# Hybrid diffusion step on one core: the low parts and sums of the feed-forward stages, sums of squares and rope product move from GpSimd to VectorE

## The chip, the cores and the metric

The kernel runs on one core of a Trainium2 chip. The metric is the device time of one execution in microseconds (us). A core has TensorE (PE, matrix products), VectorE (DVE), ScalarE (ACT), GpSimd (POOL) and SyncE (SP), which here only issues transfers. Each engine takes its instructions in a fixed order and waits at the head of its own queue.

## The reference

Two layers (DEPTH 2, width 1024) run over 256 context tokens and 1024 latent tokens. Each layer mixes attention, a recurrent unit and a long convolution, then a SwiGLU feed-forward of width 2816. Cut to what the change touches:

```python
def trunk_layer(x, mod, lp, ctx):
    sh1, sc1, g1, sh2, sc2, g2 = mod
    h = rmsnorm(x, lp['norm1_w']) * (1 + sc1) + sh1
    p = h @ lp['w_in']
    q = rmsnorm(p[..., :OFF_K].reshape(B, L, N_HEADS, HEAD_DIM), lp['q_norm_w'])
    k = rmsnorm(p[..., OFF_K:OFF_V].reshape(B, L, N_KV, HEAD_DIM), lp['k_norm_w'])
    ...
    q, k = axial_rope(q), axial_rope(k)      # latent tokens only
    ...
    x = x + g1 * (mix @ lp['w_out'])
    h2 = rmsnorm(x, lp['norm2_w']) * (1 + sc2) + sh2
    x = x + g2 * ((jax.nn.silu(h2 @ lp['ffn_w1']) * (h2 @ lp['ffn_w3'])) @ lp['ffn_w2'])
```

All data is float32.

## The kernel before

A float32 product is made of three products of reduced-precision parts (`mm3`, L154 to L156): high by high, high by low, low by high. Each operand is therefore cut in two: ScalarE copies the high part (`split`, L160, or L527), and a subtraction gives the low part (L161, or L528). Which engine subtracts is an argument. "Cut" below means such a pair, and in counts its subtraction.

The latent tokens are two blocks of 512. The feed-forward uses a fast 2x2 block scheme with seven products in place of eight. It has three pieces in each layer.

- `quarters` makes the seven operands: the normalised blocks (scaled at L507), their sums and differences (L538, L539, L546, L547), and a cut of each (`hq` holds both parts or the high ones, `hl` the low parts of three of them).
- `ffn_up` loops over 11 pairs p of weight tiles, with two parts each (w1 and w3). A part loads two `wst` tiles, cuts them and their differences into four `whl` tiles of 128x1024, makes seven products `pu` for the latent tokens and two `puv` for the context, evacuates them on VectorE (L622, L637 to L648) and applies the gate. At the end of a pair five block sums (L656) go to memory (L657); those that are named `gs` share one buffer.
- `ffn_down` runs seven stages over 11 steps each. A step loads one or two quarters of w2 into `wst` (L694), adds two at L706 where there are two, cuts the result into `whl`, loads and cuts the stored sum `gr`, and multiplies. Stages 1 and 3 (from 0) also serve the context: two more weight cuts (`C`) and one of the context's `gr` half, `gk`. Stages end with the update of `x_l` (L733).

`ss_add` (L353) adds squares for the norms, the sums with index h = 1 on GpSimd. `head_norm` (L776) normalises q and k and applies the rope: shuffle (L804), product (L805), two more steps.

Weight tiles share pools: four `whl` buffers and three `wst` buffers. The order of every engine's instructions is set by a scheduler from the order of the code and its own costs, so the change of an engine can also move other instructions.

Of the kernel before, what the change touches and what calls it, by code (L numbers as in the profile page):

```python
# [11 lines left out]
F32 = mybir.dt.float32  # L12
# [3 lines left out]
ALU = mybir.AluOpType  # L16
# [72 lines left out]
class Net:  # L89
# [261 lines left out]
    def ss_add(self, s, pool, ss, xs, d, three=3):  # L351
        nc = self.nc
        if d < 2:  # L353
            nc.scalar.activation(ss[:, d], xs, AF.Square)
        else:
            if s.lat:
                sq = pool.tile(list(xs.shape), F32, tag=self.sq[0], name="sq", bufs=self.sq[1])
            else:
                sq = self.rows(list(xs.shape))
            nc.scalar.activation(sq, xs, AF.Square)  # L360
            h = 0 if d % three == 0 else 1
            (nc.gpsimd if h else nc.vector).tensor_tensor(ss[:, h], ss[:, h], sq, ALU.add)

    def h_new(self, s, bi, hp):
        s.h[bi] = []
# [144 lines left out]
    def quarters(self, cp, cq, hp):  # L510


        nc = self.nc
        ha, hb, _ = hp
        b11, b21 = self.lat.x[0]
        b12, b22 = self.lat.x[1]
        V, G = nc.vector, nc.gpsimd

        def pair(p, tag):
            t = p.tile([128, 2, 4, 512], F32R, tag=tag, name="hq")  # L520
            return t[:, 0], t[:, 1]

        def low(tag):
            return cp.tile([128, 4, 512], F32R, tag=tag, name="hl")

        def cut(x, hl, k, eng):
            nc.scalar.activation(hl[0][:, k], x[:, k], AF.Copy)  # L527
            eng.tensor_tensor(hl[1][:, k], x[:, k], hl[0][:, k].bitcast(F32), ALU.subtract)  # L528

        h11, h21 = pair(hb, "hl00"), pair(ha, "hl01")  # L530
        for k in range(4):
            cut(b11, h11, k, G)
            cut(b21, h21, k, V)
        t1, h22 = pair(hb, "hl10"), pair(hb, "hl11")
        a, b = pair(cq, "hq1")
        c = cq.tile([128, 4, 512], F32R, tag="hq4", name="hq4")
        for k in range(4):
            V.tensor_tensor(b11[:, k], b12[:, k], b11[:, k], ALU.subtract)  # L538
            V.tensor_tensor(b12[:, k], b22[:, k], b12[:, k], ALU.subtract)  # L539
            cut(b11, t1, k, G)  # L540
        t3 = (a, low("xq00"))
        for k in range(4):
            cut(b12, t3, k, V if k % 2 else G)
        for k in range(4):
            cut(b22, h22, k, G)
            V.tensor_tensor(b22[:, k], b22[:, k], b11[:, k], ALU.subtract)  # L546
            V.tensor_tensor(b21[:, k], b22[:, k], b21[:, k], ALU.subtract)  # L547
        t2 = (b, low("xq10"))
        for k in range(4):
            cut(b22, t2, k, V)  # L550
        t4 = (c, low("xq11"))
        for k in range(4):
            cut(b21, t4, k, V if k % 2 else G)
        return h11, h21, h22, t4, t1, t2, t3

    def ffn_up(self, l, pool, cp, hq, mods):


        nc, a = self.nc, self.a
        H = NFF // 2  # L560
        lat, cs = self.lat, self.ctxs
        V, G = nc.vector, nc.gpsimd
        h11, h21, h22, t4, t1, t2, t3 = hq
        e = cp.tile([128, 4, 512], F32, tag="xq01", name="e")

        def cut(st):
            w = self.wp.tile([128, 2, 8, 128], F32R, tag="whl", name="whl", bufs=WBUFS)
            self.split(st, w[:, 0], w[:, 1], G)
            return w

        def prod(w, x, b):
# [5 lines left out]
        for p in range(H):  # L577
            ts = {}
            cps = [None, None]
            for part, src in enumerate((a["ffn_w1"][l], a["ffn_w3"][l])):  # L580
                raw = []
                for i in range(2):
                    f = p + i * H
                    st = self.wp.tile([128, 8, 128], F32, tag="wst", name="wst", bufs=SBUFS)
# [65 lines left out]
            for q, (b, op) in enumerate(BSUM):  # L650
                if len(b) == 1:
                    t = ts[b[0]]
                else:
                    n = q % 3
                    t = e[:, n + 1] if n else pool.tile([128, 512], F32, tag="gs", name="gs", bufs=1)
                    G.tensor_tensor(t, ts[b[0]], ts[b[1]], op)  # L656
                nc.sync.dma_start(lat.gd[q, p], t)  # L657
            for m in mods[2 * p:2 * p + 2]:
                self.mods(*m, self.rows, lambda nm, shp=(128, 512): self.ps_l(nm, shp, "n"))
# [1 line left out]
    def ffn_down(self, l, hp, pool, xp, last):  # L661

        nc, a = self.nc, self.a
# [20 lines left out]
        for n, (quads, op, q, outs, ctx, nxt) in enumerate(DOWN):  # L684
# [3 lines left out]
            for p in range(H):  # L688
# [12 lines left out]
                if ctx:  # L701
                    C = self.wp.tile([128, 2, 2, 512], F32R, tag="whl", name="whl", bufs=WBUFS)
                    for j in range(2):
                        self.split(st[:, j], C[:, j, 0], C[:, j, 1], nc.gpsimd)
                if len(src) == 2:
                    nc.vector.tensor_tensor(st[:, 0], st[:, 0], st[:, 1], op)  # L706
                self.split(st[:, 0], A[:, 0], A[:, 1], nc.gpsimd)
                self.split(br, B[:, 0], B[:, 1], nc.vector)
                if n < 2 and 0 < p < 9:
                    if p == 1:  # L710
# [64 lines left out]
    def head_norm(self, es, wc, pool):  # L775
        nc = self.nc  # L776
# [14 lines left out]
        for (s, bi, b0, n), e in es:  # L791
# [9 lines left out]
            if s.lat:  # L801
                cs = self.rope[b0]
                sh = pool.tile([128, n], F32, tag="qt", name="qsh", bufs=QT)
                nc.vector.stream_shuffle(sh, e, [(i + 16) % 32 for i in range(32)])  # L804
                nc.gpsimd.tensor_tensor(sh, sh, cs[:, 1], ALU.mult)  # L805
                nc.vector.tensor_tensor(e, e, cs[:, 0], ALU.mult)
                nc.vector.tensor_tensor(e, e, sh, ALU.add)
            outs.append((s, b0, n, e))
# [805 lines left out]
```

## Time and profile before

| | |
|---|---|
| runs | 3678.79, 3682.36, 3681.47 us, median 3681.47 |
| profiled execution | 3678.18 us, span 3676.4 us |
| granted TensorE clock, mean | 0.971 |
| PE busy | 3476.9 us, 95% of the span |
| DVE busy | 2331.1 us, 63% |
| ACT busy | 1430.7 us, 39% |
| POOL busy | 1444.6 us, 39% |

A busy time is the sum of the instructions of an engine. An engine that is not the last to be ready can wait at no cost, so busy shares are read stage by stage. In the first layer `quarters` ends near 1125 us, `ffn_up` runs to about 1660 and `ffn_down` to about 1955; in the second layer these are 2840, 3370 and the end. The input projection of the second layer lies between 1955 and 2250.

### The profile page before, as it was taken

The page shows a single profiled execution, that of the slowest core. Times are in us where ns is not written, and L with a number is a line of the kernel's source. Part 1 is how long each engine was busy: PE and PEld are TensorE (multiplying, and loading weights), DVE is VectorE, ACT ScalarE, POOL GpSimd, SP SyncE. Part 2 cuts the span into 40 slices and gives each one's busy share as a digit, 9 for nine tenths or more (in the row PEclk, how much of TensorE's full clock was granted, in tenths as well). Part 3 has the DMA queues.
Part 4 walks back from the last instruction along what each step waited for, and adds up shares of the span by engine and source line. Part 5 has one row for each costly group of instructions (what it writes and reads, how often), then busy time and mean ns, then how long its engine had stood idle before and what let it go on. Part 6 is the DMA issues. An engine that isn't in the chain of part 4 may idle for free.

```text
span 3676.4 us, 49838 instructions
## 1 busy us (share of the span) xinstructions
PE 3476.9 (95%) x18198; PEld 2758.4 (75%) x18198; DVE 2331.1 (63%) x4016; ACT 1430.7 (39%) x2347; POOL 1444.6 (39%) x940
## 2 busy tenths in 40 slices
PE   6989988999999999999999999989998999999998
PEld 3657776667777888887777778767686888888777
DVE  6544577887466655665685673777638556565666
ACT  4333333655342222224544542455524222222443
POOL 3333034110145555547654332310035555455664
PEclk7999998999999999999999999999998999999999
DMA  7565573310411222226675336430141222224667
GB/s 273 175 202 164 201 277 107 121 48 23 138 52 63 89 78 92 78 90 231 191 238 182 106 117 203 153 108 28 36 151 36 84 92 78 77 92 157 205 205 244
DMA packets 402331, 485.89 MB, mean 132 GB/s; under 512 B 38542, under 2 KB 251072, under 8 KB 398758
## 3 DMA queue, kind: packets, MB, share of 16 engines
q1 hardware_dynamic: 398950, 468.03, 38.7%
q0 software_dynamic: 3136, 14.68, 1.2%
q8 instruction: 143, 2.34, 0.3%
q14 instruction: 102, 0.84, 0.1%
HBM read 350.94 MB, written 131.67 MB: 131 GB/s over the span
## 4 chain that ended last, share of the span: by engine, by line
PE 60%; DVE 7%; DMA 6%; issue 5%; POOL 4%; ACT 2%; SPq 1%; DVEq 0%; POOLq 0%; ACTq 0%
PE pu L155 8%; PE pu L156 8%; PE pu L154 8%; PE pvo L966 4%; PE sps L931 4%; PE tps L947 4%; POOL whl L161 3%; PE puv L155 2%; PE puv L154 2%; PE puv L156 2%; PE ops L155 2%; PE ops L156 2%; PE ops L154 2%; DMA wst<-in_ffn_w_dram 2%; PE py L154 2%
## 5 line engine op out<-in xcount | busy, mean ns | idle before, releaser
L161 POOL TENSOR_TENSOR whl<-wst,whl 128x512 fp32r<-128x512 f32 (+1 forms) x463 | 898.3, 1950 | 866.5 <-ACT whl L160 833.6
L160 ACT ACTIVATE whl<-wst 128x512 fp32r<-128x512 f32 (+1 forms) x488 | 394.2, 825 | 846.2 <-PE pu L156 277.9
L154 PE MATMUL pu<-hq,whl 128*128 128x512 f32 x1232 | 489.6, 399 | 7.6 <-ACT hq L527 6.2
L156 PE MATMUL pu<-hq,whl 128*128 128x512 f32 x1232 | 488.8, 398 | 0.0
L154 PE MATMUL wps<-h,whl 128*128 128x512 f32 (+1 forms) x768 | 289.3, 377 | 2.9 <-ACT h L404 1.7
L155 PE MATMUL pu<-hq,whl 128*128 128x512 f32 x704 | 280.8, 399 | 8.4 <-POOL hq L528 4.8
L156 PE MATMUL wps<-h,whl 128*128 128x512 f32 (+1 forms) x768 | 287.9, 376 | 0.0
L155 PE MATMUL wps<-h,whl 128*128 128x512 f32 (+1 forms) x768 | 285.0, 371 | 1.7 <-POOL h L161 1.2
L154 PEld LDWEIGHTS pu<-hq,whl 128*128 128x128 f32 x1232 | 234.1, 190 | 63.0 <-ACT hq L527 8.1
L156 PEld LDWEIGHTS pu<-hq,whl 128*128 128x128 f32 x1232 | 234.4, 190 | 54.9
L154 PE MATMUL py<-whl 128*128 128x512 f32 x616 | 225.1, 399 | 14.3 <-ACT whl L160 8.9
L155 PE MATMUL py<-whl 128*128 128x512 f32 x616 | 228.5, 395 | 0.1
L156 PE MATMUL py<-whl 128*128 128x512 f32 x616 | 220.5, 394 | 1.6 <-POOL whl L161 1.6
L155 PE MATMUL pu<-hl,whl 128*128 128x512 f32 x528 | 210.9, 400 | 8.8 <-POOL hl L528 8.8
L934 ACT ACTIVATE pq<-pq,mn 128x1280 f32<-128x1280 f32 (+1 forms) x160 | 190.2, 1189 | 66.3 <-DVE pq L932 64.0
L947 PE MATMUL tps<-ident,pq 128*128 128x128 f32 x1344 | 198.7, 279 | 16.0 <-ACT pk L951 6.2
L156 PE MATMUL puv<-h,whl 128*128 128x256 f32 x704 | 200.4, 285 | 4.6 <-POOL whl L161 4.6
L154 PE MATMUL puv<-h,whl 128*128 128x256 f32 x704 | 200.1, 284 | 1.4 <-ACT whl L160 1.4
L706 DVE TENSOR_TENSOR wst<-wst 128x512 f32<-128x512 f32 x110 | 137.1, 1247 | 99.5 <-POOL whl L161 63.4
L155 PE MATMUL puv<-h,whl 128*128 128x256 f32 x704 | 200.0, 284 | 0.0
L947 PEld LDWEIGHTS tps<-ident,pq 128*128 128x128 f32 x1344 | 158.4, 143 | 52.4 <-DVE pk L949 18.1
L932 DVE TENSOR_SCALAR_CACHE_REDUCE pq<-sps,mn 128x512 f32<-128x512 f32 (+1 forms) x256 | 156.4, 612 | 46.7 <-PE sps L931 43.2
(355 smaller groups left out, 8038.1 us busy)
## 6 DMA issues: line engine op xcount, KB each, us to landing
wst<-in_ffn_w_dram SPq DMA_DIRECT2D x264, 256.0 KB
wst<-in_ffn_w_dram SPq DMA_DIRECT2D x88, 512.0 KB
wst<-in_w_mod_dram SPq DMA_DIRECT2D x68, 512.0 KB
gr<-gd_l SPq DMA_DIRECT2D x132, 256.0 KB
gd_l<-gs SPq DMA_DIRECT2D x66, 256.0 KB
wst<-in_w_in_dram SPq DMA_DIRECT2D x32, 512.0 KB
wst<-in_w_mod_dram SPq DMA_DIRECT2D x14, 1024.0 KB
gd_l<-g SPq DMA_DIRECT2D x44, 256.0 KB
```

The lines of the kernel that those rows point to most:

```text
L154: mm(ps, wh, xh, start=first, stop=False)
L155: mm(ps, wh, xl, start=False, stop=False)
L156: mm(ps, wl, xh, start=False, stop=last)
L160: nc.scalar.activation(hi, src, AF.Copy)
L161: (eng or nc.vector).tensor_tensor(lo, src, hi.bitcast(F32), ALU.subtract)
L706: nc.vector.tensor_tensor(st[:, 0], st[:, 0], st[:, 1], op)
L931: nc.tensor.matmul(p, qx[:, ts], kt[:, h, k0:k0 + kn], start=h == 0, stop=h == 1)
L932: nc.vector.tensor_scalar(pt[:, k0:k0 + kn], p, -1.0, mn[:, c - 1:c] if c else BIG, ALU.mult, ALU.min, accum_out=mn[:, c:c + 1])
L934: nc.scalar.activation(pt, pt, AF.Exp, bias=mn[:, len(chunks) - 1:], scale=-1.0, accum_out=ls[:, t:t + 1])
L947: nc.tensor.transpose(ps[:, k, t], pq[t][:, (t0 + k) * 128:(t0 + k + 1) * 128], self.ident)
L966: nc.tensor.matmul(ob[64 * hd:64 * hd + 64, 0], vx[:, t], pk[:, t].rearrange("p t q -> p (t q)"), start=t == nkt - 1, stop=t == 0)
```

## The change

Seven sites get VectorE in place of GpSimd: the sums of squares with h = 1, all cuts of `quarters`, the weight cuts and block sums of `ffn_up`, the weight cuts of `ffn_down`, and the rope product. Nothing is computed in another way. GpSimd keeps the weight cuts of the input and output projections, half of the cuts of the first norm's result, and the recurrent unit's, the convolution's and the filters' work.

```diff
@@ ss_add
-            (nc.gpsimd if h else nc.vector).tensor_tensor(ss[:, h], ss[:, h], sq, ALU.add)
+            nc.vector.tensor_tensor(ss[:, h], ss[:, h], sq, ALU.add)
@@ quarters
-        def cut(x, hl, k, eng):
+        def cut(x, hl, k):
             nc.scalar.activation(hl[0][:, k], x[:, k], AF.Copy)
-            eng.tensor_tensor(hl[1][:, k], x[:, k], hl[0][:, k].bitcast(F32), ALU.subtract)
+            V.tensor_tensor(hl[1][:, k], x[:, k], hl[0][:, k].bitcast(F32), ALU.subtract)
...
-            cut(b11, t1, k, G)
+            cut(b11, t1, k)
...
-            cut(b12, t3, k, V if k % 2 else G)
+            cut(b12, t3, k)
@@ ffn_up
-            self.split(st, w[:, 0], w[:, 1], G)
+            self.split(st, w[:, 0], w[:, 1])
...
-                    G.tensor_tensor(t, ts[b[0]], ts[b[1]], op)
+                    V.tensor_tensor(t, ts[b[0]], ts[b[1]], op)
@@ ffn_down
-                        self.split(st[:, j], C[:, j, 0], C[:, j, 1], nc.gpsimd)
+                        self.split(st[:, j], C[:, j, 0], C[:, j, 1])
...
-                self.split(st[:, 0], A[:, 0], A[:, 1], nc.gpsimd)
+                self.split(st[:, 0], A[:, 0], A[:, 1])
@@ head_norm
-                nc.gpsimd.tensor_tensor(sh, sh, cs[:, 1], ALU.mult)
+                nc.vector.tensor_tensor(sh, sh, cs[:, 1], ALU.mult)
```

Three places in VectorE's order show what moves. In the first, `quarters` of layer 0, right after the last scaling L507, VectorE had only the sums of the blocks:

```order
L538 TENSOR_TENSOR xq_8660<-xq_8682,xq_8660 128x512 x3
L539 TENSOR_TENSOR xq_8682<-xq_8683,xq_8682 128x512
L538 TENSOR_TENSOR xq_8660<-xq_8682,xq_8660 128x512
L539 TENSOR_TENSOR xq_8682<-xq_8683,xq_8682 128x512 x2
L546 TENSOR_TENSOR xq_8683<-xq_8683,xq_8660 128x512
```

After the change the same place holds a weight cut and the cuts L528 between those sums:

```order
L161 TENSOR_TENSOR whl<-wst,whl 128x1024
L538 TENSOR_TENSOR xq_8660<-xq_8682,xq_8660 128x512 x2
L528 TENSOR_TENSOR hq<-xq_8683,hq 128x512
L538 TENSOR_TENSOR xq_8660<-xq_8682,xq_8660 128x512
L528 TENSOR_TENSOR hq<-xq_8683,hq 128x512
L538 TENSOR_TENSOR xq_8660<-xq_8682,xq_8660 128x512
L539 TENSOR_TENSOR xq_8682<-xq_8683,xq_8682 128x512
L528 TENSOR_TENSOR hq<-xq_8683,hq 128x512
L539 TENSOR_TENSOR xq_8682<-xq_8683,xq_8682 128x512
```

The xq names are the four quarter blocks, two for each token block. Twenty cuts and one weight cut now share the queue with the 16 sums, where GpSimd ran 12 of the cuts and that weight cut.

The second place is the end of a pair in `ffn_up` of layer 0. VectorE went from the gate (L614) straight to the evacuations of the next pair's products:

```order
L634 TENSOR_TENSOR wst<-wst 128x512
L614 SCALAR_TENSOR_TENSOR g<-g,e 128x512
L622 TENSOR_TENSOR g<-pu,e 128x512
L612 SCALAR_TENSOR_TENSOR g<-e,g 128x512
L637 TENSOR_TENSOR e<-pu,e 128x512
L639 TENSOR_TENSOR g<-pu,e 128x512
```

After the change the block sums L656 and the weight cuts stand between them:

```order
L656 TENSOR_TENSOR gs<-g 128x512
L614 SCALAR_TENSOR_TENSOR g<-g,e 128x512 x2
L656 TENSOR_TENSOR e<-g 128x512
L656 TENSOR_TENSOR gs<-g 128x512
L656 TENSOR_TENSOR e<-g 128x512
L622 TENSOR_TENSOR g<-pu,e 128x512
L161 TENSOR_TENSOR whl<-wst,whl 128x1024
L656 TENSOR_TENSOR gs<-g 128x512
L612 SCALAR_TENSOR_TENSOR g<-e,g 128x512
L161 TENSOR_TENSOR whl<-wst,whl 128x1024
```

Five sums, three of them in the one `gs` buffer, and two weight cuts now stand around the first evacuation L622 of the next pair.

The third place is a step of `ffn_down` in its first context stage. VectorE had three or four instructions a step, of which these five rows show one and the beginning of the next:

```order
L161 TENSOR_TENSOR whl<-gr,whl 128x512
L706 TENSOR_TENSOR wst<-wst 128x512
L161 TENSOR_TENSOR gk<-gr,gk 128x512
L161 TENSOR_TENSOR whl<-gr,whl 128x512
L706 TENSOR_TENSOR wst<-wst 128x512
```

After the change a step has six, with the three weight cuts in a row:

```order
L706 TENSOR_TENSOR wst<-wst 128x512
L161 TENSOR_TENSOR gk<-gr,gk 128x512
L161 TENSOR_TENSOR whl<-gr,whl 128x512
L161 TENSOR_TENSOR whl<-wst,whl 128x512 x3
L706 TENSOR_TENSOR wst<-wst 128x512
```

The three cuts that formed GpSimd's whole queue there now stand between the cut of `gr` and the next sum L706.

## Rows read from the trace of the kernel before

**Rows 1.** The page, part 1: engine, busy us, share, instructions.

```profile
PE 3476.9 (95%) x18198; PEld 2758.4 (75%) x18198; DVE 2331.1 (63%) x4016; ACT 1430.7 (39%) x2347; POOL 1444.6 (39%) x940
```

**Rows 2.** Windows, one a stage: length, then busy us by engine, clock, DMA share, GB/s.

```profile
1090.00:1125.00 35.00, 22.79 (x84) 17.57 (x85) 32.02 (x34) 17.63 (x30) 22.41 (x14) 0.71 0.01 4
1125.00:1660.00 535.00, 535.00 (x2769) 454.48 (x2768) 325.83 (x370) 133.90 (x176) 276.43 (x138) 1.00 0.26 86
1690.00:1730.00 40.00, 36.58 (x151) 27.52 (x150) 27.40 (x27) 18.81 (x36) 30.16 (x22) 1.00 0.64 212
1830.00:1850.00 20.00, 16.08 (x68) 12.41 (x67) 11.78 (x13) 8.01 (x15) 9.68 (x8) 1.00 0.48 161
1850.00:1960.00 110.00, 103.83 (x461) 84.11 (x460) 101.29 (x142) 55.94 (x100) 68.22 (x46) 0.97 0.75 246
1960.00:2250.00 290.00, 269.78 (x1357) 220.12 (x1358) 159.83 (x243) 128.95 (x197) 87.11 (x48) 0.95 0.41 134
2800.00:2840.00 40.00, 26.58 (x102) 19.77 (x101) 35.57 (x41) 19.97 (x33) 23.55 (x14) 0.74 0.01 4
3410.00:3440.00 30.00, 27.47 (x114) 21.06 (x115) 19.09 (x16) 14.21 (x27) 23.36 (x16) 1.00 0.58 185
3550.00:3560.00 10.00, 6.50 (x27) 4.68 (x26) 8.16 (x7) 3.52 (x7) 6.73 (x5) 1.00 0.23 80
```

**Rows 3.** Groups by line and form, POOL, whole span: busy us, mean ns, idle before.

```profile
L161 POOL TENSOR_TENSOR whl<-wst,whl 128x1024 fp32r<-128x1024 f32 x221 | 550.7, 2493 | 627.5 <-ACT whl L160 603.4 <-issue 20.5 <-DMA fe_l<-e 3.6
L161 POOL TENSOR_TENSOR whl<-wst,whl 128x512 fp32r<-128x512 f32 x242 | 347.7, 1454 | 239.0 <-ACT whl L160 230.2 <-DMA gr<-gd_c 5.2 <-issue 1.3
L656 POOL TENSOR_TENSOR gs<-g 128x512 f32<-128x512 f32 x66 | 86.1, 1305 | 88.2 <-DVE g L614 87.8 <-DMA gd_l<-gs 0.4
...
L805 POOL TENSOR_TENSOR qsh<-qsh,cs 128x512 f32<-128x512 f32 x20 | 33.5, 1677 | 106.4 <-DVE qsh L804 77.1 <-PE wps L156 9.8 <-DMA wst<-in_w_in_dram 9.5
```

**Rows 4.** Timeline of DVE, 1085 to 1126: start, us, instruction (merged: xcount).

```profile
1087.83 5.36 DVE L507 SCALAR_TENSOR_TENSOR xq<-xq,nA,nps 128x512 f32<-128x512 f32 x8 [1.57 <-PE nps L389]
...
1095.95 1.76 DVE L539 TENSOR_TENSOR xq<-xq,xq 128x512 f32<-128x512 f32 x1
...
1107.23 0.41 DVE L598 SCALAR_TENSOR_TENSOR gc<-gc,puv 128x256 f32<-128x256 f32 x1
...
1109.70 0.68 DVE L546 TENSOR_TENSOR xq<-xq,xq 128x512 f32<-128x512 f32 x1
...
1114.48 3.81 DVE L528 TENSOR_TENSOR hl<-xq,hq 128x512 fp32r<-128x512 f32 x6
```

**Rows 5.** Timeline of POOL, 1085 to 1126.

```profile
1110.60 3.41 POOL L528 TENSOR_TENSOR hl<-xq,hq 128x512 fp32r<-128x512 f32 x2 [5.04 <-issue]
...
1120.97 2.97 POOL L528 TENSOR_TENSOR hl<-xq,hq 128x512 fp32r<-128x512 f32 x2
```

**Rows 6.** Waits of PE, 1085 to 1125: us in total, times, longest.

```profile
PE pu L155 <- POOL hl L528: 4.3, 1, 4.3
```

**Rows 7.** Timeline of POOL, 1690 to 1730.

```profile
1701.41 4.70 POOL L161 TENSOR_TENSOR whl<-wst,whl 128x512 fp32r<-128x512 f32 x3 [1.29 <-ACT whl L160]
1707.40 4.70 POOL L161 TENSOR_TENSOR whl<-wst,whl 128x512 fp32r<-128x512 f32 x3 [1.29 <-ACT whl L160]
```

**Rows 8.** Waits of SP's queue, whole span: us in total, times, longest.

```profile
SPq L694 <- POOL whl L161: 113.0, 82, 5.1
```

**Rows 9.** Groups by line and form, DVE, whole span.

```profile
L637 DVE TENSOR_TENSOR e<-pu,e 128x512 f32<-128x512 f32 x44 | 30.4, 692 | 229.1 <-PE pu L156 229.1
...
L622 DVE TENSOR_TENSOR g<-pu,e 128x512 f32<-128x512 f32 x22 | 15.2, 691 | 100.2 <-POOL gs L656 100.2
```

**Rows 10.** Groups by line and form, DVE, 1850 to 1960.

```profile
L706 DVE TENSOR_TENSOR wst<-wst 128x512 f32<-128x512 f32 x30 | 34.2, 1139 | 3.1 <-DMA wst<-in_ffn_w_dram 2.9
L161 DVE TENSOR_TENSOR whl<-gr,whl 128x512 fp32r<-128x512 f32 x31 | 31.9, 1040 | 4.0 <-ACT whl L160 4.0
```

**Rows 11.** Groups by line and form, POOL, 1850 to 1960.

```profile
L161 POOL TENSOR_TENSOR whl<-wst,whl 128x512 fp32r<-128x512 f32 x31 | 46.7, 1515 | 36.7 <-ACT whl L160 34.9 <-issue 1.3 <-PE py L156 0.2
```

More of the change, by code (lines that the diff above doesn't have):

```diff
@@ L516, in quarters @@
         b12, b22 = self.lat.x[1]
-        V, G = nc.vector, nc.gpsimd
+        V = nc.vector
         def pair(p, tag):
@@ L524, in low @@
             return cp.tile([128, 4, 512], F32R, tag=tag, name="hl")
-        def cut(x, hl, k, eng):
+        def cut(x, hl, k):
             nc.scalar.activation(hl[0][:, k], x[:, k], AF.Copy)
-            eng.tensor_tensor(hl[1][:, k], x[:, k], hl[0][:, k].bitcast(F32), ALU.subtract)
+            V.tensor_tensor(hl[1][:, k], x[:, k], hl[0][:, k].bitcast(F32), ALU.subtract)
         h11, h21 = pair(hb, "hl00"), pair(ha, "hl01")
         for k in range(4):
-            cut(b11, h11, k, G)
-            cut(b21, h21, k, V)
+            cut(b11, h11, k)
+            cut(b21, h21, k)
         t1, h22 = pair(hb, "hl10"), pair(hb, "hl11")
@@ L539, in quarters @@
             V.tensor_tensor(b12[:, k], b22[:, k], b12[:, k], ALU.subtract)
-            cut(b11, t1, k, G)
+            cut(b11, t1, k)
         t3 = (a, low("xq00"))
         for k in range(4):
-            cut(b12, t3, k, V if k % 2 else G)
+            cut(b12, t3, k)
         for k in range(4):
-            cut(b22, h22, k, G)
+            cut(b22, h22, k)
             V.tensor_tensor(b22[:, k], b22[:, k], b11[:, k], ALU.subtract)
@@ L549, in quarters @@
         for k in range(4):
-            cut(b22, t2, k, V)
+            cut(b22, t2, k)
         t4 = (c, low("xq11"))
         for k in range(4):
-            cut(b21, t4, k, V if k % 2 else G)
+            cut(b21, t4, k)
         return h11, h21, h22, t4, t1, t2, t3
```

## The prediction, made before the changed kernel ran

> **What bounds the kernel now.** I read the engine totals first. TensorE is busy 95% of the span and VectorE 63% [rows 1], so the time can only fall where TensorE stands idle, about 200 us in all. The table by stage says where that is. In the feed-forward up stage TensorE is busy for all of its 535 us [rows 2], so faster side work there is worth nothing. It idles at its two ends. In the 35 and 40 us ahead of it, where `quarters` prepares the operands, 12.2 us (35.00 − 22.79) and 13.4 us (40.00 − 26.58) are idle, and the granted clock is 0.71 and 0.74 of full. In feed-forward down the idle pieces are 3.4 and 2.5 us in the first stage that also serves the context (1690 to 1730, 3410 to 3440) and 3.9 and 3.5 us where the second such stage hands over to the next (1830 to 1850, 3550 to 3560). 1850 to 1960 has 6.2 us more, and the input projection of layer 1 (1960 to 2250) 20.2 us.
>
> Next I read the durations. On GpSimd a moved instruction on 128x512 takes 1.31 to 1.68 us and one on 128x1024 2.49 us [rows 3]. On VectorE the same form has two prices. The sums of `quarters` take 1.76 us while GpSimd runs its own subtractions, 0.68 us alone, and six subtractions in a row take 3.81 us, 0.635 us each [rows 4]. I use 0.635 us for each moved 128x512 instruction and 1.27 us for each 128x1024 one.
>
> **The change, part by part.** No instruction is added. 625 move from GpSimd to VectorE: 45 sums of squares, 32 cuts of `quarters`, 176 weight cuts and 110 block sums of `ffn_up`, 242 weight cuts of `ffn_down`, and 20 rope products.
>
> *Quarters.* Let T be the start of the last eight scalings at L507 (1087.83) [rows 4]. The last low part is done at 1120.97 + 2.97 = 1123.94, T + 36.1, and the first one of the first `hl` tile at about 1110.60 plus half of 3.41, 1112.3, T + 24.5 [rows 5]. After the change everything stands in VectorE's one queue: eight scalings (5.36), one 128x1024 weight cut (1.27), 16 sums and 20 cuts (36 × 0.635 = 22.9) and two small gate steps (2 × 0.41) [rows 4], together T + 30.3. 15 sums and eight cuts stand ahead of the first `hl`: 5.36 + 1.27 + 23 × 0.635 + 0.8, and its own 0.635, give T + 22.7. So the first operand comes 1.8 us earlier and the last 5.8 us. TensorE waits 4.3 us for an `hl` low part from GpSimd [rows 6], which lies between them. I take 3 us in each layer, **−6** (bounds −3.6 and −11.6). T itself stays: ahead of it VectorE gets four more cuts and loses stretched ones.
>
> *Feed-forward up.* VectorE is busy 325.8 of 535 us and GpSimd 276.4 [rows 2]. A moved instruction shrinks by 0.635/1.31 to 1.27/2.49, about 0.49, so at most 135 us come on top: 461 of 535 us, 86%, even if VectorE's own work stays as stretched as now. TensorE has no idle to give back: **0**. One wait is new. The sum `gs` at L656 has one buffer, so it waits for the store of the sum before; behind it on VectorE stand the evacuation L622 and the weight cuts for the next part. Today only GpSimd stands there. The cover is VectorE's lead: it idles 229.1 us over 44 parts, 5.2 us a part, ahead of L637, where it waits for TensorE, and 100.2 us at L622 for the sums that GpSimd makes late [rows 9].
>
> *Feed-forward down, first context stage.* GpSimd runs three cuts a step, 4.70 us, then stands 1.29 us, with steps 5.99 us apart (1701.41 to 1707.40) [rows 7], longer than what TensorE works in one: 36.58/40 × 5.99 = 5.5 us. After the change the three cuts, L706, the cut of `gr` and that of `gk` are six VectorE instructions, 3.8 us, so TensorE sets the step. All of the idle goes: 3.4 + 2.5 = **−6** (0 if the loads set the step).
>
> *Hand-over at 1830 and 3550.* SyncE waits 113.0 us, 82 times, at L694 for GpSimd's cuts to free a `wst` buffer before it can load the next weights [rows 8]. A cut that is 1.45 − 0.635, 0.8 us, shorter [rows 3, 4] and not queued behind two others lets the loads start sooner. The load itself remains, so of 3.9 and 3.5 us I take 2.5 each, **−5** (bounds 0 and −7.4).
>
> *1850 to 1960.* 31 weight cuts come onto VectorE [rows 11], 19.7 us. It is busy 101.3 of 110 us now [rows 2], but its 30 instructions of L706 average 1139 ns and its 31 cuts of `gr` 1040 ns [rows 10], 0.50 and 0.41 us over the price alone, 28 us in all. So 101 + 20 − 28 = 93 us. I take **0** (bounds −6.2, all idle gone, and +11 below).
>
> *Rope products and sums of squares.* 20 products go from 1677 to 635 ns, 21 us if each were on the path. GpSimd spends most of its idle ahead of them waiting for VectorE's shuffle [rows 3], and VectorE has the next product to do anyway. Of the 20.2 us of idle in layer 1's projection I take **−4** with the sums of squares (0 to −8).
>
> Sum: −6 + 0 − 6 − 5 + 0 − 4 = **−21 us**. The profiled run took 3678.18 us, 3.3 below the median 3681.47. So the profile should come to 3657 and the median to **3660**. The scheduler also sets some VectorE rows in another order, which I price at ±4, the size of one of the terms. About 0.2%, 7.4 us, is what a measurement of this kernel can tell from no change.
>
> **A rule weighed.** On 1850 to 1960 the rows say 101.3 us busy with 28 us of stretch in it. The Trainium skill, Perfetto Trace Analysis, section "Optimizing Scalar/DVE Operations", says that a saturated VectorE may hand work to ScalarE or even GpSimd, while warning that this may not help because the two share an SBUF port. By its first half the change goes the wrong way in this stretch, and the sum would be −10 instead of −21; by its second half it stays −21. The trace bears out the second.
>
> **The rivals.**
> 1. *VectorE becomes the bound at 1850 to 1960.* If its stretch does not go, because GpSimd keeps the cuts of the normalised input and of the next layer's weights there, 101.3 + 19.7 is 121 us of work in 110: +11, 3671 in the median. For it: 92% busy now. Against it: the 0.68 us in rows 4.
> 2. *Slower: the queue in feed-forward up.* A moved load of 135/22 = 6.1 us a part stands against the 5.2 us lead at L637. If VectorE's other idle lies where the moved cuts cannot run, because they stand behind `gs` waiting for its store or behind an evacuation, TensorE loses 0.9 us in each of 44 parts, +40, 3700. It decides from (21 + 7.4)/44 = 0.65 us a part. For it: one queue now holds what TensorE needs next and what it has just finished. Against it: the 0.68 us prices would shorten VectorE's own stretched steps, and idle of 9.5 us a part (209/22) exceeds 6.1.
> 3. *Nothing.* The starts of the stages are set by the norm ahead of T and by loads, not by cuts; each gain is taken up by the next wait: 3675 to 3688. For it: TensorE's waits ahead of the up stage are split over ScalarE, GpSimd and VectorE, none over 4.3 us. Against it: the 5.99 us steps repeat.
> 4. *More.* The idle of all the named pieces in the feed-forward goes: 12.2 + 13.4 + 3.4 + 2.5 + 3.9 + 3.5 + 6.2 = 45 us, 3636. Against it: 30.3 us of VectorE's queue still stand between T and the last operand.
>
> **How the numbers follow.** Forecast 0.52, rival 1 0.08, rival 2 0.18, rival 3 0.13, rival 4 0.09. The forecast's own range is 3648 to 3670. Low end 3640 leaves out most of rival 4; high end 3686 leaves out most of rival 2 and holds rivals 1 and 3. Faster: forecast, rival 4 and 0.05 of rival 1, whose time lies near the bound, 0.66. Same: rival 3 and the rest of rival 1, 0.16. Slower: 0.18.
>
> **What would show it.** Right: VectorE's sums at L538 to L547 and L706 near 0.68 us; the stretch from the last L507 to the end of the last `hl` cut near 25 us instead of 31; TensorE full from 1690 to 1730 and 3410 to 3440; shorter waits of SyncE at L694; feed-forward up still near 535 us. Wrong: TensorE waiting in feed-forward up for VectorE's `whl` cuts or for its evacuations, `gs` waiting for its own store, or VectorE above 95% at 1850 to 1960.

## The result, and the profile after

The changed kernel takes 3634.82 us in the median of 4 runs (3629.33 to 3638.75), the kernel before 3680.13 us in the runs beside it: a ratio of 0.9877, interval 0.9862 to 0.9892. That is 45 us faster, where 21 were forecast, and 5 us below the low end of the range. The profiled execution took 3633.1 us; its span is 45.1 us shorter than the 3676.4 us of the kernel before.

The engine totals of the changed kernel, the line that answers to [rows 1]:

```profile
PE 3459.9 (95%) x18198; PEld 2752.3 (76%) x18198; DVE 2430.4 (67%) x4641; ACT 1437.6 (40%) x2347; POOL 384.9 (11%) x315
```

The reader should take three numbers from it. TensorE is busy 17.0 us less (3476.9 to 3459.9) for the same 18198 matmuls, so it idles only 28.1 us less; together these are the 45.1. VectorE has 625 instructions more and is busy only 99 us more. The weight cuts alone that it got are 176 of 1.27 us and 242 of 0.635, 377 us by the price of the prediction, so the work that it had before shrank by over 270 us.

The stages, with the same columns as in [rows 2]; the windows of feed-forward down and of layer 1 are set to the time at which the stage now runs:

```profile
1090.00:1125.00 35.00, 23.14 (x87) 17.93 (x86) 32.42 (x53) 20.57 (x33) 0.00 (x0) 0.80 0.01 4
1125.00:1655.00 530.00, 530.00 (x2761) 451.00 (x2760) 346.72 (x501) 135.83 (x173) 0.00 (x0) 1.00 0.27 85
1690.00:1730.00 40.00, 39.53 (x171) 31.71 (x171) 30.58 (x50) 20.87 (x37) 0.00 (x0) 1.00 0.75 240
1820.00:1840.00 20.00, 19.64 (x84) 15.30 (x83) 12.60 (x21) 9.55 (x17) 0.00 (x0) 1.00 0.52 166
1840.00:1945.00 105.00, 101.43 (x460) 82.12 (x459) 93.78 (x173) 53.54 (x95) 11.42 (x8) 0.98 0.80 265
1945.00:2235.00 290.00, 276.59 (x1463) 227.81 (x1462) 176.01 (x276) 136.22 (x210) 74.68 (x43) 0.99 0.45 149
2766.00:2806.00 40.00, 27.71 (x114) 21.69 (x113) 37.37 (x64) 21.56 (x35) 0.00 (x0) 0.83 0.01 4
3372.00:3402.00 30.00, 30.00 (x131) 24.30 (x130) 22.14 (x36) 15.88 (x29) 0.00 (x0) 1.00 0.68 211
3510.00:3520.00 10.00, 8.93 (x38) 6.79 (x37) 5.60 (x9) 3.46 (x6) 0.00 (x0) 1.00 0.52 171
```

Feed-forward up is still full. The two context stages, 3.4 and 2.5 us idle before, have 0.5 and 0 idle; the hand-overs have 0.4 and 1.1 in place of 3.9 and 3.5. From 1840 VectorE is busy 93.8 of 105 us, 89%, and TensorE idles 3.6 us in place of 6.2. Ahead of the up stage TensorE idles nearly as long as before in a window of the same length, 11.9 and 12.3 us, but at a granted clock of 0.80 and 0.83 in place of 0.71 and 0.74. In layer 0 that window starts 4.6 us earlier against T than before, so the whole stage, further down, is the better measure. In layer 1's projection the clock is 0.99 in place of 0.95.

VectorE through `quarters` of layer 0, which answers to [rows 4]:

```profile
1092.47 5.36 DVE L507 SCALAR_TENSOR_TENSOR xq<-xq,nA,nps 128x512 f32<-128x512 f32 x8 [4.16 <-PE nps L389]
1097.75 1.22 DVE L161 TENSOR_TENSOR whl<-wst,whl 128x1024 fp32r<-128x1024 f32 x1
1098.88 1.29 DVE L538 TENSOR_TENSOR xq<-xq,xq 128x512 f32<-128x512 f32 x2
...
1104.30 1.29 DVE L528 TENSOR_TENSOR hq<-xq,hq 128x512 fp32r<-128x512 f32 x2
...
1116.39 5.11 DVE L528 TENSOR_TENSOR hl<-xq,hq 128x512 fp32r<-128x512 f32 x8
```

T is now 1092.47. The sums take 0.69 us and the low parts end at 1121.5, T + 29.0 (T + 36.1 before, T + 30.3 forecast). The weight cut behind the eight scalings is a new wait for TensorE, seen between 1090 and 1126; the longest one for GpSimd's weight cut there was 1.9 us before:

```profile
PE puv L156 <- DVE whl L161: 5.4, 1, 5.4
```

Groups of VectorE over the whole span, which answer to [rows 9] and [rows 10], and SyncE's wait, which answers to [rows 8]:

```profile
L161 DVE TENSOR_TENSOR whl<-gr,whl 128x512 fp32r<-128x512 f32 x132 | 90.9, 690 | 7.7 <-ACT whl L160 7.6
...
L706 DVE TENSOR_TENSOR wst<-wst 128x512 f32<-128x512 f32 x110 | 75.9, 690 | 36.7 <-DMA wst<-in_ffn_w_dram 36.6
...
L656 DVE TENSOR_TENSOR gs<-g 128x512 f32<-128x512 f32 x66 | 45.5, 689 | 54.3 <-DMA gd_l<-gs 54.3
...
L637 DVE TENSOR_TENSOR e<-pu,e 128x512 f32<-128x512 f32 x44 | 30.1, 684 | 1.7 <-PE pu L156 1.7
...
L622 DVE TENSOR_TENSOR e<-pu,e 128x512 f32<-128x512 f32 x22 | 15.2, 692 | 41.0 <-PE pu L156 41.0
L622 DVE TENSOR_TENSOR g<-pu,e 128x512 f32<-128x512 f32 x22 | 15.2, 691 | 4.2 <-DVE e L656 2.2 <-ACT whl L160 1.8
```

```profile
SPq L694 <- DVE whl L161: 165.0, 112, 13.2
```

L706 went from 1247 ns over the whole span to 690, the cuts of `gr` from 1021 to 690. The 229.1 us that VectorE idled for TensorE ahead of L637 are 1.7 now; idle of 41.0 us stands ahead of an L622 instead, and 54.3 us ahead of `gs` for its own store, as the new wait of the prediction said. TensorE waits for none of it. SyncE's wait at L694 did not shrink: 165.0 us for VectorE's cuts where it was 113.0 for GpSimd's and 24.1 for VectorE's own. TensorE idles less all the same, so that sign of the prediction told nothing.

In the first context stage the step is now 5.57 us in place of 5.99, near the 5.5 of TensorE's own work that the prediction named:

```profile
1712.83 0.68 DVE L706 TENSOR_TENSOR wst<-wst 128x512 f32<-128x512 f32 x1
...
1718.40 0.68 DVE L706 TENSOR_TENSOR wst<-wst 128x512 f32<-128x512 f32 x1
```

At the hand-over the trace names the wait that ended TensorE's idle, between 1828 and 1852 before and between 1815 and 1842 after:

```profile
PE pyc L156 <- DVE gk L161: 3.9, 2, 2.3
```

```profile
PE pyc L156 <- DVE gk L161: 0.3, 1, 0.3
```

It is VectorE's own cut of the context's `gk`, no weight and no load. In layer 1 the same wait goes from 3.5 to 1.1 us.

To place the 45 us I compare the time of the same instruction in two traces: the last scaling L507 of a layer (4.6 us behind T; the column "to T" ends there), the first and last `py` matmul, the first evacuation of the projection (L444) and the first score matmul `sps`. The differences between neighbours give each stage's gain. Two executions of one program set the scale: e5 below repeats the kernel before.

| gain in us by stage (minus is faster) | to T, layer 0 | quarters + up, 0 | down, 0 | gap | projection, 1 | mixer, 1 | quarters + up, 1 | down, 1 | sum |
|---|---|---|---|---|---|---|---|---|---|
| changed kernel | +4.7 | −5.0 | −14.5 | −1.0 | −14.9 | −2.0 | −4.5 | −8.1 | −45.3 |
| e5, before again | +1.9 | 0.0 | −0.6 | +0.7 | −1.3 | −0.2 | −0.3 | +4.0 | +4.2 |
| e1, quarters | −4.6 | −4.9 | −0.3 | −0.5 | +3.5 | −4.5 | −4.9 | +3.9 | −12.3 |
| e2, up | +2.8 | −0.4 | −0.4 | −0.7 | −10.1 | −2.1 | −0.4 | −2.0 | −13.3 |
| e3, down | +0.7 | −0.2 | −8.8 | +1.9 | −0.5 | −2.5 | +0.3 | −4.3 | −13.4 |
| e4, rope and squares | +1.8 | −0.6 | +1.4 | +2.9 | −14.8 | −0.3 | −0.6 | +1.7 | −8.5 |
| e6, layer 1 alone | +5.3 | −0.2 | +0.2 | 0.0 | −1.6 | −0.1 | −4.5 | −5.9 | −6.8 |
| e7, GpSimd repeats | +5.2 | +13.9 | +8.4 | +2.3 | −10.0 | −1.7 | +14.3 | +8.9 | +41.3 |
| e8, all but up | −0.2 | −5.4 | −12.3 | −1.0 | −10.7 | −2.6 | −5.2 | −4.4 | −41.8 |
| e9, all but rope | +8.1 | −5.1 | −11.2 | −1.0 | 0.0 | −3.7 | −4.6 | −7.8 | −25.3 |
| e10, more | +8.3 | −4.9 | −12.8 | +0.4 | −19.3 | −4.4 | −4.7 | −11.2 | −48.6 |
| e11, most | +10.7 | −4.9 | −9.3 | −2.3 | −11.7 | 0.0 | −4.8 | −6.8 | −29.1 |
| e12, down and squares | +2.9 | −0.2 | −8.7 | −0.8 | +1.6 | +0.9 | 0.0 | −4.8 | −9.1 |

Each row is one profiled execution, so its sum may stand some us from the median of that kernel's runs.

Whole stages in the columns of [rows 2], before and then after: quarters with the up stage and down of layer 0, then of layer 1.

```profile
1092.40:1655.30 562.90, 551.63 (x2825) 466.76 (x2824) 351.44 (x397) 147.70 (x199) 292.72 (x149) 0.98 0.25 80
1655.30:1956.60 301.30, 286.19 (x1237) 229.02 (x1237) 220.08 (x266) 145.20 (x260) 197.02 (x139) 0.99 0.68 223
2806.50:3369.00 562.50, 551.72 (x2826) 466.20 (x2826) 351.42 (x397) 147.43 (x199) 292.59 (x149) 0.98 0.25 80
3369.00:3669.00 300.00, 287.02 (x1271) 230.75 (x1270) 196.90 (x226) 129.08 (x226) 177.17 (x123) 0.99 0.69 226
```

```profile
1097.10:1655.00 557.90, 550.20 (x2831) 466.84 (x2832) 374.51 (x546) 151.50 (x199) 0.00 (x0) 0.99 0.25 81
1655.00:1941.80 286.80, 282.40 (x1237) 228.47 (x1236) 226.61 (x392) 144.38 (x257) 8.22 (x7) 0.99 0.72 236
2773.80:3331.80 558.00, 549.81 (x2831) 466.45 (x2832) 374.67 (x546) 151.48 (x200) 0.00 (x0) 0.99 0.25 81
3331.80:3623.70 291.90, 285.38 (x1271) 229.91 (x1270) 214.19 (x349) 129.07 (x226) 0.00 (x0) 1.00 0.71 233
```

A stage's time is TensorE's busy time and its idle time. Quarters with up give back 6.2 us of idle and 3.3 of busy time over both layers, down 17.2 and 5.4.

### The profile page after: what moved, and what is told of

Read it like the earlier page. It is cut to its first block, busy times and chain, and to the rows that moved or that the text cites. A ratio compares the mean times of both kernels' runs of the same rounds, so it can differ in the third digit from the quotient of the medians.

```text
span 3631.3 us, 49329 instructions
## 1 busy us (share of the span) xinstructions
PE 3459.9 (95%) x18198; PEld 2752.3 (76%) x18198; DVE 2430.4 (67%) x4641; ACT 1437.6 (40%) x2347; POOL 384.9 (11%) x315
## 5 line engine op out<-in xcount | busy, mean ns | idle before, releaser
L161 DVE TENSOR_TENSOR whl<-wst,whl 128x512 fp32r<-128x512 f32 (+1 forms) x443 | 394.7, 905 | 278.6 <-ACT whl L160 276.1
L155 PE MATMUL py<-whl 128*128 128x512 f32 x616 | 226.4, 395 | 2.0 <-DVE whl L161 1.9
L154 PE MATMUL py<-whl 128*128 128x512 f32 x616 | 219.9, 396 | 3.8 <-DVE x_l L733 2.3
L156 PE MATMUL py<-whl 128*128 128x512 f32 x616 | 214.4, 394 | 2.8 <-DVE whl L161 2.8
L156 PE MATMUL puv<-h,whl 128*128 128x256 f32 x704 | 200.7, 285 | 10.7 <-DVE whl L161 10.7
L932 DVE TENSOR_SCALAR_CACHE_REDUCE pq<-sps,mn 128x512 f32<-128x512 f32 (+1 forms) x256 | 156.0, 611 | 44.6 <-PE sps L931 40.8
L154 PEld LDWEIGHTS wps<-h,whl 128*128 128x128 f32 x768 | 146.6, 191 | 45.5 <-issue 11.0
```

Source lines behind the costliest of these rows:

```text
L154: mm(ps, wh, xh, start=first, stop=False)
L155: mm(ps, wh, xl, start=False, stop=False)
L156: mm(ps, wl, xh, start=False, stop=last)
L161: (eng or nc.vector).tensor_tensor(lo, src, hi.bitcast(F32), ALU.subtract)
L932: nc.vector.tensor_scalar(pt[:, k0:k0 + kn], p, -1.0, mn[:, c - 1:c] if c else BIG, ALU.mult, ALU.min, accum_out=mn[:, c:c + 1])
```

## The experiments

Theory A says that each place gives back what TensorE lost there, and that places add up. Theory B says that what counts is GpSimd's silence, since the two engines block each other. Theories C to E are about single stages.

**e5: the kernel before once more.** No edit.

> The kernel before, profiled once more, as the measure of how far a stage's time moves between two executions of the same program. If stages repeat within 2 us, the 10 us that the up-stage variant gained in layer 1's projection, where it moved no instruction, come from the order that the scheduler gave there. If the projection moves by 5 us or more between two executions, they are chance.

One run, 3682.35 us. Six of the eight stages repeat within 1.3 us, the start within 1.9, the last stage moves by 4.0. The kernels e1, e2, e3 and e6, which change nothing ahead of `quarters`, show −4.6 to +5.3 in the start, so that stage moves by 5 us and is not argued on.

**e1: quarters alone.**

```diff
-            eng.tensor_tensor(hl[1][:, k], x[:, k], hl[0][:, k].bitcast(F32), ALU.subtract)
+            V.tensor_tensor(hl[1][:, k], x[:, k], hl[0][:, k].bitcast(F32), ALU.subtract)
```

> The kernel before with only the 32 cuts of quarters on VectorE. Theory A (each place gives back its own TensorE idle time, and the places add up): about -10 us, as from the start of the last scalings to the first matmul of feed-forward down the two layers gained 4.7 us (5.0 and 4.5) in the changed kernel. Theory B (the gain needs GpSimd silent: a VectorE instruction beside a GpSimd one takes 1.75 us in place of 0.68): one weight cut of 2.4 us and the sums of squares stay on GpSimd, VectorE's longer queue runs into them, and the gain is under 4 us.

3667.24 us against 3682.13, ratio 0.9960 (0.9946 to 0.9973), −15 us. The stage from the last scalings to the first `py` gains 4.9 us in both layers, as in the changed kernel. Theory A holds for this place, theory B's loss does not appear: moving these 16 cuts a layer by itself leaves GpSimd only weight cuts there. The other 5 of the 15 us are not in this place; in the profile they lie in the start and the mixer, and were not explained.

**e2: feed-forward up alone.**

```diff
-            self.split(st, w[:, 0], w[:, 1], G)
+            self.split(st, w[:, 0], w[:, 1], V)
...
-                    G.tensor_tensor(t, ts[b[0]], ts[b[1]], op)
+                    V.tensor_tensor(t, ts[b[0]], ts[b[1]], op)
```

> The kernel before with only the weight cuts and the block sums of feed-forward up on VectorE. Theory A: TensorE is busy for all of the 535 us before and after, so 0, within 4 us. Rival (VectorE's queue delays TensorE there, hidden in the full change by the gains of the other places): +5 to +40 us.

3660.62 us, ratio 0.9937 (0.9924 to 0.9949), −21 us, where both theories are wrong in the whole. In its own stages it gains 0.4 us in each layer, as theory A says, so the fuller VectorE queue costs TensorE nothing there and the rival falls. The profiled execution gains 10.1 us in layer 1's projection, where no instruction changed its engine. That execution, 3664.72 us, is the slowest of the five, so the table shows only 13.3 of the 21 us.

**e3: feed-forward down alone.**

```diff
-                        self.split(st[:, j], C[:, j, 0], C[:, j, 1], nc.gpsimd)
+                        self.split(st[:, j], C[:, j, 0], C[:, j, 1])
...
-                self.split(st[:, 0], A[:, 0], A[:, 1], nc.gpsimd)
+                self.split(st[:, 0], A[:, 0], A[:, 1])
```

> The kernel before with only the weight cuts of feed-forward down on VectorE. Theory A: the two layers' stages gained 14.5 and 8.0 us in the changed kernel, so -22 us. Theory B: sums of squares stay on GpSimd beside a fuller VectorE, so the stages 4 to 6 lose what the stages 1 to 3 gain: about -10 us.

3669.85 us, ratio 0.9966 (0.9953 to 0.9979), −12 us; its stages gain 8.8 and 4.3. That is near the 11 us that the prediction gave this part, and below the 22.6 of the changed kernel.

**e4: rope product and sums of squares alone.**

```diff
-            (nc.gpsimd if h else nc.vector).tensor_tensor(ss[:, h], ss[:, h], sq, ALU.add)
+            nc.vector.tensor_tensor(ss[:, h], ss[:, h], sq, ALU.add)
...
-                nc.gpsimd.tensor_tensor(sh, sh, cs[:, 1], ALU.mult)
+                nc.vector.tensor_tensor(sh, sh, cs[:, 1], ALU.mult)
```

> The kernel before with only the rope product and the sums of squares on VectorE. Theory A (a shorter rope chain): layer 1's projection gained 15 us and the mixer behind it 2 us more in the changed kernel, layer 0's projection nothing or -5, so -10 to -17 us in all. Theory C (layer 1's projection gained because GpSimd comes free of the feed-forward cuts, so that the cuts it keeps there start in time): 0 to -4 us here.

3676.17 us, ratio 0.9983 (0.9974 to 0.9991), −6 us. The projection of layer 1 gains 14.8 us, as in the changed kernel, and some of it is lost again in other stages. Theory C falls, since GpSimd keeps all feed-forward cuts here.

**e6: the feed-forward sites of layer 1 alone.** Each site picks its engine by the layer, shown at one of them:

```diff
-            self.split(st, w[:, 0], w[:, 1], G)
+            self.split(st, w[:, 0], w[:, 1], V if l else G)
```

> All feed-forward sites moved in layer 1 alone, so that nothing ahead of 2785 us changes, the projection of layer 1 included. Theory A (each place gives back its own idle time): quarters with the up stage -4.5, feed-forward down -8, -12 us in all. Theory D (most of the whole gain comes from the order that the scheduler made anew in the projection): still -12 here, but then the same sites in layer 0 with the rest make up the remaining 33 us. If parts interact by contention only (theory B), -8 or less.

3668.48 us against 3679.92, ratio 0.9969 (0.9957 to 0.9980), −11.4 us; −4.5 in quarters and up and −5.9 in down. Theory A's −12 holds.

**e7: the changed kernel with GpSimd subtracting beside it.** GpSimd reads a high part and writes a tile that nobody reads; the same in `ffn_down` with the weight's high part:

```diff
             V.tensor_tensor(hl[1][:, k], x[:, k], hl[0][:, k].bitcast(F32), ALU.subtract)
+            r = hl[0][:, k].bitcast(F32)
+            nc.gpsimd.tensor_tensor(gp.tile([128, 512], F32, tag="gs", name="scr", bufs=1), r, r, ALU.subtract)
...
+                r = A[:, 0].bitcast(F32)
+                nc.gpsimd.tensor_tensor(pool.tile([128, 512], F32, tag="scr", name="scr", bufs=1), r, r, ALU.subtract)
```

> The changed kernel, in which GpSimd also subtracts the high part from itself into a scratch tile that nobody reads, once for each cut of quarters (28 a layer) and for each step of feed-forward down (77 a layer). Nothing waits for it. Theory B (VectorE and GpSimd block each other, so that GpSimd's silence is what shortens VectorE): quarters' sums and cuts go from 0.69 to over 1 us on average, the stretch from the last scalings to the last low part from 29 to 36 us or more, and the whole is 15 to 40 us slower than the changed kernel, -30 to -5 us against the kernel before. Theory A (only the moved instructions' own shorter time and place in a queue count): as fast as the changed kernel, -45 us, within 4.

3717.85 us, ratio to the kernel before 1.0103 (1.0087 to 1.0118): 83 us slower than the changed kernel, beyond even theory B's price. Every moved instruction runs on VectorE as in the changed kernel, and in `quarters` and the up stage VectorE, ScalarE and TensorE keep its order in both layers; further on some rows stand elsewhere. GpSimd gets 28 subtractions a layer in `quarters`, where it had 16 before the change, and 77 in down, where it had 121, so e7 shows the mechanism and not the price of the change. VectorE in `quarters` of layer 0 (lines are two or more below those of the changed kernel: L540 is its L538):

```profile
1092.95 5.36 DVE L507 SCALAR_TENSOR_TENSOR xq<-xq,nA,nps 128x512 f32<-128x512 f32 x8 [3.11 <-PE nps L389]
1098.22 1.51 DVE L161 TENSOR_TENSOR whl<-wst,whl 128x1024 fp32r<-128x1024 f32 x1
1099.65 2.97 DVE L540 TENSOR_TENSOR xq<-xq,xq 128x512 f32<-128x512 f32 x2
1102.54 1.52 DVE L528 TENSOR_TENSOR hq<-xq,hq 128x512 fp32r<-128x512 f32 x1
...
1108.32 0.68 DVE L541 TENSOR_TENSOR xq<-xq,xq 128x512 f32<-128x512 f32 x1
```

GpSimd at the same time:

```profile
1093.13 14.72 POOL L530 TENSOR_TENSOR scr<-hq 128x512 f32<-128x512 f32 x11 [32.42 <-PE nps L389]
```

And TensorE's largest wait there:

```profile
PE pu L155 <- DVE hl L528: 10.8, 3, 8.5
```

The sums take 1.52 us and start 1.45 us apart while GpSimd runs 11 of its own, 1.34 us each; a sum in a pause of GpSimd takes 0.68 (1108.32). The eight scalings L507, which read one operand from PSUM, keep their 5.36 us although GpSimd starts 0.2 us behind them. The last low part is done at about T + 48 in place of T + 29. Quarters and up lose 18.9 and 18.8 us against the changed kernel, down 22.9 and 17.0. Theory B is right about the mechanism: beside GpSimd work that reads SBUF, VectorE's two-input instructions advance about one for each of GpSimd's. The weight's high part is also held until GpSimd has read it, so not all of the loss in down need be this.

**e8: all but the up stage.**

> The change without the weight cuts and the block sums of feed-forward up. Theory A with places that add up: the up stage alone gave -21.5 us, so this gives -45 + 21.5 = -24. Sum of the other three parts measured alone: -33. Theory D (the part alone gained by a new order in the projection, which the rope and sums of squares also bring): -40 to -45.

The edit is the diff of the change without its two `ffn_up` lines. 3639.35 us, ratio 0.9891 (0.9873 to 0.9909), −40.6 us. So the up stage is worth about 4.5 us inside the whole, where the two intervals still overlap, and 21 alone; the rest of its 21 us is had without it. Parts do not add up. The totals of this execution, with VectorE carrying 286 instructions fewer than in the changed kernel:

```profile
PE 3464.6 (95%) x18198; PEld 2749.7 (76%) x18198; DVE 2388.0 (66%) x4355; ACT 1430.1 (39%) x2347; POOL 966.6 (27%) x601
```

**e9: all but the rope product.**

```diff
+                nc.gpsimd.tensor_tensor(sh, sh, cs[:, 1], ALU.mult)
-                nc.vector.tensor_tensor(sh, sh, cs[:, 1], ALU.mult)
```

> The change without the rope product. Every instruction of layer 1's projection then stands in the order of the kernel before, with the product on GpSimd. If layer 1's projection gains by the rope product and the order that comes with it: 0 there within 3 us, and -45 + 15 = -30 in all. If it gains because GpSimd and VectorE come out of the feed-forward stages less loaded: -10 or more there, and -40 to -45 in all.

3653.62 us against 3679.99, ratio 0.9923 (0.9911 to 0.9936), −26.4 us. The projection of layer 1 gains 0.0. So the rope product, with the order that it brings, is what the projection's 15 us hang on, and the −30 that goes with it is near. The relief of the feed-forward stages ahead of it brings nothing there.

The same 1359 matmuls of that projection (L444's first to the first `sps`) in the kernel before, and 40 us of it; then in e5, e9, e2, e4 and the changed kernel, with the columns of [rows 2]:

```profile
1989.00:2267.50 278.50, 261.12 (x1359) 214.70 (x1359) 152.04 (x228) 123.72 (x189) 79.83 (x45) 0.96 0.44 145
2160.00:2200.00 40.00, 31.89 (x156) 27.35 (x155) 29.85 (x49) 16.67 (x25) 11.85 (x6) 0.83 0.36 117
```

```profile
1991.30:2268.20 276.90, 259.96 (x1359) 213.49 (x1358) 152.56 (x229) 123.54 (x189) 79.39 (x44) 0.98 0.44 145
```

```profile
1980.10:2258.30 278.20, 261.72 (x1358) 215.22 (x1358) 152.39 (x228) 123.69 (x189) 79.33 (x44) 0.96 0.44 145
```

```profile
1990.60:2258.70 268.10, 256.89 (x1359) 210.35 (x1359) 152.76 (x228) 123.72 (x189) 79.83 (x44) 0.99 0.46 150
```

```profile
1994.80:2258.20 263.40, 255.40 (x1358) 211.23 (x1358) 155.09 (x239) 122.79 (x189) 62.76 (x34) 0.99 0.46 153
```

```profile
1973.50:2236.80 263.30, 254.38 (x1359) 209.87 (x1359) 154.41 (x239) 122.49 (x189) 63.48 (x34) 0.99 0.46 153
2134.00:2174.00 40.00, 37.95 (x210) 32.60 (x209) 33.03 (x54) 17.18 (x27) 10.40 (x5) 1.00 0.49 162
```

Before, again and e9: 278.5, 276.9, 278.2 us, with the clock at 0.96 to 0.98. e4 and after: 263.4 and 263.3, at 0.99. In e2 VectorE is busy 152.8 and GpSimd 79.8 us, as before (152.0 and 79.8), the products stay on GpSimd, and the stage takes 268.1 at 0.99. There at least 29 of VectorE's 228 instructions, 38 of ScalarE's 189 and 109 of TensorE's stand in another place than in the kernel before. So a new order alone can be worth 10 of the 15 us. The order of e4's and of the changed kernel's projection is one and the same, that of e9 and of the kernel before another; between these two at least 70 of TensorE's own instructions have another place. Over all the traces the gain goes with the order: e3, e5, e6, e9 and e12 have that of the kernel before and stand within 1.6 us of it, e1, which differs in a few rows, at +3.5; every kernel with another order gains 10.0 to 19.3 (e10 and e11 also move more cuts there). Among those, e7 and e8 have the product on VectorE and gain 10.0 and 10.7, and e2 has it on GpSimd and gains 10.1. So no trace shows a gain from the product's engine itself. What the product's engine is worth in an unchanged order stays open: it wasn't tried, since the scheduler orders anew with every change of engine.

What the order acts on shows in part in the 40 us at 2160 to 2200, beside 40 us around the same wait after the change; by the other order the two stretches hold 156 and 210 matmuls. TensorE's wait in the kernel before for the stretch 2100 to 2240, and in the changed one:

```profile
PE qp L799 <- ACT qrx L795: 6.1, 1, 6.1
```

```profile
PE qp L799 <- ACT qrx L795: 2.0, 1, 2.0
```

One wait for ScalarE's copy of the norm factors (`qrx`, L795) shrinks from 6.1 to 2.0 us. Over those 40 us the granted clock is 0.83 before, a mean over stretches at 1.2 and at 2.4 GHz, and 1.00, all at 2.4 GHz, after. The low stretches lie at the end of two gaps of TensorE and behind them, the 6.1 us to 2167 and one of 2.0 us to 2188; four us at each stand at 0.50, so 1.2 GHz:

```profile
2164.00:2168.00 4.00, 1.22 (x6) 1.22 (x7) 2.00 (x3) 1.89 (x2) 1.60 (x1) 0.50 0.00 0
2188.00:2192.00 4.00, 4.00 (x14) 3.42 (x15) 0.39 (x2) 1.46 (x3) 0.00 (x0) 0.50 0.62 222
```

The wait for `qrx` in the changed kernel, 2.0 us to 2143, left the clock at 1.00.

**e10: the weight cuts of the projections on VectorE too.**

```diff
-        self.split(st, w[:, 0], w[:, 1], eng or nc.gpsimd)
+        self.split(st, w[:, 0], w[:, 1], eng)
```

> The changed kernel with the weight cuts of the input and output projections on VectorE too, 45 of 128x1024. Theory B (GpSimd's silence shortens VectorE): the projections lose the stretch that GpSimd's 2.5 us cuts cause, another -5 to -15 us, -50 to -60 against the kernel before. Theory A alone (a moved cut pays only where TensorE waits for it): TensorE waits 0.5 to 3 us for those cuts in a projection, so -45 within 4.

3635.40 us, ratio 0.9883 (0.9868 to 0.9898), −44.6: no faster than the changed kernel. Theory A's −45 holds. VectorE takes 45 more instructions and is busy 12.5 us more than in the changed kernel:

```profile
PE 3459.9 (95%) x18198; PEld 2746.9 (76%) x18198; DVE 2442.9 (67%) x4686; ACT 1439.1 (40%) x2347; POOL 273.6 (8%) x270
```

**e11: the low parts of the first norm's result too.**

```diff
-                self.split(t, hh, hl, nc.gpsimd)
+                self.split(t, hh, hl)
```

> As the kernel of the run before, with the low parts of the first norm's result on VectorE too, 32 of them. TensorE waits 1.6 us for one of them in the changed kernel. Theory B: a few us more than the run before, -50 to -65 against the kernel before. Rival: VectorE, already 90% busy at the end of feed-forward down in layer 0, becomes the bound there: no faster than the run before, or slower by up to 5 us.

3642.93 us, ratio 0.9900 (0.9886 to 0.9914), −37.1: 7.5 us slower than e10 in the median, with intervals that overlap. Theory B's few us more did not come; that it is slower than e10 is not clear of the noise. Down in layer 0 gains 9.3 us here and 12.8 in e10, the projection of layer 1, whose order is another one again, 11.7 and 19.3. The rival's place, down in layer 0, is thus not the larger part, and the rest was not separated.

**e12: feed-forward down with the sums of squares.**

> The kernel before with the weight cuts of feed-forward down and the sums of squares on VectorE. Feed-forward down alone (cuts without sums) gained 8.8 and 4.3 us in its two layers, with all the rest moved but the rope product 11.2 and 7.8. Theory E (the sums of squares that stay on GpSimd beside a fuller VectorE cost the difference): 11 and 8 us here, -18 us in all. Rival (the difference comes from quarters and the up stage, which leave a better start): 9 and 4 as with the cuts alone, -12 in all.

The edit is that of e3 with the first line of e4. 3667.19 us against 3682.49, ratio 0.9956 (0.9942 to 0.9969), −15.3 us. Its stages gain 8.7 and 4.8 us, as in e3. Theory E falls.

## Why the prediction was wrong

**The step that failed first** is the premise that "the time can only fall where TensorE stands idle". Of the 45.1 us, 28.1 are idle time, against 21 forecast, and 17.0 are busy time, which the sum put at nothing. That is the larger part of the 24 us by which the gain was missed. The busy time fell most in the projection (6.7 us, clock 0.96 to 0.99); it also fell in down of layer 0 (3.8 us), where the clock reads 0.99 before and after, so there the reason is not shown.

**The rope term was mis-sized: −4, measured −15.** The step said that VectorE "has the next product to do anyway" and took 4 of the 20.2 us of idle. e9 and e4 show 0.0 and −14.8 in the projection without and with that edit. Two things were mis-sized. The scheduler's new order, priced at ±4 as noise, was worth 10 us in e2 in the same stage. And the sum counted TensorE's idle time only: the clock went from 0.96 to 0.99 there and the same matmuls took 6.7 us less of busy time (261.1 to 254.4), beside 8.5 us less idle (17.4 to 8.9).

**Feed-forward down was mis-sized: −11 and 0, measured −22.6.** The context stages lost 5.5 us of idle, where 6 were forecast, and the step fell to TensorE's own, as forecast. The hand-overs lost 6.0, where 5 were forecast, but by another way: the prediction named loads held up by GpSimd's cuts at L694, while TensorE waited for VectorE's cut of `gk` (3.9 us, then 0.3) and SyncE's wait at L694 grew. The size was luck there. That cut went from 883 to 690 ns with the rest of VectorE's two-input work; what else brought it forward was not separated. Beyond these places down gave back 5.7 us more of idle and 5.4 of busy time. L706 and the cuts of `gr` went to 0.69 us, and e3, with these cuts alone, gave 13.1 us. The other 9 us come only with the rest of the change; e12 shows that it is not the sums of squares. In layer 1 e5's 4.0 us in the same stage covers most of it, and e3, e8 and e12, which lack the up stage's edit and have one order there, gain 4.3 to 4.8, while the changed kernel, e6, e9, e10 and e11, with that edit and one other order, gain 5.9 to 11.2. For layer 0 (−8.8 alone, −9.3 to −14.5 with the rest, −0.6 in e5; e9 and the changed kernel differ by 3.3 with the same order) the cause stays open. "0" for 1850 to 1960 was too little: idle there fell from 6.2 to 3.6 us.

**Quarters: −6 forecast, −9.5 measured, within its bounds.** T + 29.0 against T + 30.3 forecast. All kernels that have this edit and no added GpSimd work gain 4.5 to 5.4 us a layer, e1 alone included. Idle time fell by 6.2 us over both layers, as forecast; the other 3.3 us are busy time again, with the clock at 0.99 in place of 0.98. The queue of the forecast left out one wait: the weight cut behind the scalings holds TensorE up for 5.4 us.

**Feed-forward up: 0 forecast, right in place.** e2 shows −0.4 a layer. The block sum's wait for its store came (54.3 us) and was covered. Rival 2 falls.

**VectorE as the bound at 1850 to 1960** (rival 1) did not come: 93.8 of 105 us, against 93 of 110 forecast. The rule of the Trainium skill's Perfetto Trace Analysis, "Optimizing Scalar/DVE Operations", that a saturated VectorE may hand work to GpSimd, would have kept the cuts where they were; its own warning, that this might not help since the two share a port, agrees with e7, where VectorE's sums took 1.52 us beside GpSimd and 0.68 in its pause.

**Rival 4**, 45 us, has the right size by another way: it named idle time in the feed-forward stages alone, and these gave back 23.4 us of it. That the total agrees is luck.

**Contention** was in the prediction as a price (0.68 against 1.76 us) and is now shown as a cause by e7. The Trainium skill, SBUF — State Buffer, section "Who interferes with whom", says that a VectorE instruction with two SBUF inputs contends with a GpSimd instruction that reads SBUF, and one with at most one SBUF input, outside the 2-port performance modes, does not. e7's rows agree: 1.52 us for the sums, 5.36 us for the eight scalings with one PSUM operand.

## What to carry to other kernels

Price an engine beside its neighbour: where VectorE and GpSimd both subtract tiles in SBUF, VectorE ran its two-input instructions at 1.5 to 1.8 us in place of 0.69, so the moved work, some 500 us on VectorE (176 cuts of 1.27 us and 449 instructions of 0.635 or, on smaller tiles, less, by the prediction's prices), added 99 us to VectorE's busy time. Count a removed TensorE gap twice where the clock was low behind it, once as idle and once as slow work. Where a scheduler orders anew with each edit, repeat the unchanged kernel to learn a stage's own spread, and look for gains in stages that the edit doesn't touch before adding up parts: here the parts alone sum to 55 us and the whole is 45.

## What the runs showed of the hardware that had not been expected

Under a steady stream of GpSimd subtractions VectorE's two-input instructions started 1.45 us apart, close to GpSimd's 1.34 us each, so VectorE fell to the pace of the slower engine and not to a share of its own (e7). And the clock: the same 1359 matmuls of a projection took 254.4 us of busy time at 0.99 of full clock and 261.1 at 0.96, with no matmul added or taken away, though partly in another order.
